# A trunk layer's first microseconds: raw x turned ahead of its norm, and the last x tile moved behind the first modulation

## The chip, the cores and the metric

One core of a Trainium2 chip runs the whole program. The time is the device time of that core in microseconds (us). The kernel before was timed in three runs. The engines are called TensorE (PE), VectorE (DVE), ScalarE (ACT), GpSimd (POOL) and SyncE (SP); SP issues nearly all transfers.

## What is computed

One layer of a hybrid backbone for 640 tokens of width 1024: 128 context tokens and 512 latent ones. Cut to what the change touches:

```python
def rms_norm(x, g):
    xf = x.astype(jnp.float32)
    y = xf * lax.rsqrt(jnp.mean(xf * xf, axis=-1, keepdims=True) + EPS)
    return (y * g.astype(jnp.float32)).astype(x.dtype)

def trunk_layer(h, ada, p, rope_tabs, ctx_k, ctx_v):
    sh1, sc1, g1, sh2, sc2, g2 = jnp.split(ada, N_ADA, axis=-1)
    u = rms_norm(h, p["g_pre1"]) * (1 + sc1) + sh1
    mo, k, v = mixer(u, p, rope_tabs, ctx_k, ctx_v)
    h = h + g1 * rms_norm(mo, p["g_post1"])
    u = rms_norm(h, p["g_pre2"]) * (1 + sc2) + sh2
    h = h + g2 * rms_norm(conv_ffn(u, p), p["g_post2"])
    return h, k, v
```

Here `ada` is silu(c) @ w_ada + b_ada, and the mixer begins with z = u @ w_in. All numbers are 32-bit floats. Products that must be exact to that are made of three products of parts: a weight or an activation is split into a high part (rounded to a narrower format, names in `whi`, `UH`) and the low rest (`wlo`, `UL`), and high x high, high x low and low x high are added up.

## The kernel before

TensorE contracts over the 128 partitions, so the modulated u is needed with features on the partitions and tokens along the row: `UH` and `UL`, eight feature blocks f of 128 features by 640 tokens. x comes from memory the other way round, in five tiles t of 128 tokens by 1024 features (`XT`; tile 0 is the context, 1 to 4 are latent).

What happens to x, ahead of the first matmul with real weights (called the prologue here):

- `square(t)`: ScalarE squares the tile and sums each row; GpSimd makes the factor 1/sqrt(mean + EPS) of it in two small steps (`rstd_of`, lines 224 and 225), one number for each token, that is for each partition.
- `normal(t)`: VectorE multiplies the tile by that factor (line 358).
- `x_turn(t)`: TensorE turns the product in eight transposes of 128x128 into PSUM (line 365).
- `x_copy(t, half)`: VectorE or ScalarE copies each half to `xT` (lines 371 and 373).

Beside this stands the modulation. Scale and shift of a feature block are sums over w_ada. Its columns are loaded in groups g (`GROUPS`: the feature blocks 0; 1; 2 and 3; 4 and 5; 6; 7), `ada1_mm(g, i)` multiplies them (i = 0 is the scale, i = 1 the shift; line 383), `ada1_copy` takes the result from PSUM on ScalarE (line 390, tile `e`), and `ada1_fold` adds up its four partial rows on TensorE (line 397) and makes `scsh` on VectorE (lines 400 and 402). `modulate(f, a, b)` then makes `UH` on ScalarE (line 417), the same in full precision on VectorE (`u`, line 418) and `UL` (line 421) for the tokens a to b. `features` and `feature_columns` turn the small vectors (c, biases, gains) into columns; the first needs four small loads that ScalarE issues.

With a modulated block f and a weight block f of w_in (K and V columns, "unit" f, split by `split`, lines 148 and 149, which `cut_upto` calls), `kv_mm(f, ts)` adds block f to the K/V result of the token tiles ts: three matmuls of 128x512 each (lines 183 to 185). `kv_first` does the same for block 0 and three tiles, ordered so that the low parts are needed last (line 428).

The order on TensorE, ScalarE, VectorE and SP is the order of the calls in the text: the engines' programs are written out by hand, and each is worked through in that order, so an instruction that waits holds up all that stands behind it on its engine. SP issues the loads in their order in the text, and at most eight are under way; the places freed by x tiles 0 to 4 take later w_ada groups (`ada_loads(2, ...)`, `ada_loads(3, ...)`). PSUM tiles come from two rings: three of two banks (`ps2`: the turned tiles, then the K/V results) and two of one bank (`ps1`: `wps` for the first transposes, `features`, then each `ada1_mm` group).

At the very start 28 transposes of the identity run on TensorE (`WARM`, line 298).

After the last `kv_mm` come attention, the convolution, the merge and the feed-forward part, in which nothing is edited.

Of the kernel before, what the change touches and what calls it, by code (L numbers as in the profile page):

```python
# [11 lines left out]
F32 = mybir.dt.float32  # L12
F32R = mybir.dt.float32r
AF = mybir.ActivationFunctionType
ALU = mybir.AluOpType
# [22 lines left out]
OFF = 192  # L38
BLKS = ((0, 320), (320, 640))
ZB = 4  # L40
XB = 4
WARM = 28
SEGS = ((0, NCTX), (NCTX, NTOK))


# [18 lines left out]
def trunk_layer(ctx, tc, x_prompt, x_sample, cache_k, cache_v, c, c_ctx, w_ada, b_ada, g_pre1, g_post1, g_pre2,  # L64
# [29 lines left out]
    def nm(s):  # L94
        cnt[0] += 1
        return f"{s}_{cnt[0]}"
# [19 lines left out]
    def ps2():  # L116
        return ps.tile([128, 1024], F32, tag="s2", name=nm("s2"), bufs=3)
# [36 lines left out]
    def fetch(i):  # L154
        while len(state["raw"]) < min(i, len(units), state["limit"]):
            w, k0, nk, c0, n = units[len(state["raw"])]
            if nk * n > 512:
                raw = raw_tile()
            else:

                if not halves:
                    raw = raw_tile()
                    halves.extend([raw[:, 512:1024], raw[:, 0:512]])
                raw = halves.pop()
            nc.sync.dma_start(raw[:, :nk * n].rearrange("p (k c) -> p k c", c=n),
                              w[k0 * 128:(k0 + nk) * 128, c0:c0 + n].rearrange("(k p) c -> p k c", p=128))
            state["raw"].append(raw)
# [125 lines left out]
    with tc.tile_pool(name="pro", bufs=2) as pro, tc.manual_schedule(engines={mybir.EngineType.SP}):  # L293
        warm = pro.tile([128, 1], F32, name="warm", bufs=1)
        S.activation(warm, mhalf[:, 0:1], AF.Silu)
        wps = ps1()
        for _ in range(WARM):
            PE.transpose(wps[:, 0:128], ident, ident)

        def load_rows(srcs, eng):  # L300
            rows = pro.tile([72, 128], F32, tag="rows", name=nm("rows"), bufs=2)
# [13 lines left out]
        def araw_tile():  # L315
            return pro.tile([128, 1024], F32, tag="araw", name=nm("araw"), bufs=4)

        def ada_loads(g, rooms):
            n, c = len(GROUPS[g]), GROUPS[g][0] * 128
            araws[g] = rooms  # L320
            for i, raw in enumerate(rooms):
                o, k = (D, 0)[i // n], i % n * (KT // n)
                nc.sync.dma_start(raw.rearrange("p (k c) -> p k c", c=128 * n),
                                  w_ada[k * 128:(k + KT // n) * 128, o + c:o + c + 128 * n].rearrange("(k p) c -> p k c", p=128))

        XT = region(ra, "r3", [NT, D], F32, "XT")
        for t in range(NT):
            nc.sync.dma_start(XT[:, t, :], xrows(t))
        ada_loads(0, [araw_tile() for _ in range(2)])
        fetch(1)  # L330
        ada_loads(1, [araw_tile() for _ in range(2)])
        fetch(2)

        def features():
            ptr = ps1()
            PE.transpose(ptr[:, 0:72], rows1, ident[0:72, 0:72])
            S.activation(svec[:, :, 30], ptr[:, 0:8], AF.Silu)
            S.activation(svec[:, :, 31], ptr[:, 8:16], AF.Silu)
            return ptr

        def feature_columns():
            V.tensor_copy(feat[:, 0:72], ptr1[:, 0:72])
            for o in (8, 32):
                V.tensor_scalar(out=feat[:, F_B + o:F_B + o + 8], in0=feat[:, F_B + o:F_B + o + 8], scalar1=1.0, scalar2=None,
                                op0=ALU.add)

        xT = Halves(NTOK, F32, "xT")
        xns, rs, xps, pas, es = {}, {}, {}, {}, {}

        def square(t):  # L350
            junk = pro.tile([128, D], F32, tag="junk", name=nm("junk"), bufs=1)
            ssq = pro.tile([128, 1], F32, tag="ssq", name=nm("ssq"), bufs=NT)
            S.activation(junk, XT[:, t, :], AF.Square, accum_out=ssq)
            rs[t] = rstd_of(ssq, 1, 1.0 / D, pro)

        def normal(t):
            xns[t] = pro.tile([128, D], F32, tag="xn", name=nm("xn"), bufs=XB)
            V.tensor_scalar(out=xns[t], in0=XT[:, t, :], scalar1=rs[t], scalar2=None, op0=ALU.mult)

        def x_turn(t, ks=range(KT)):  # L360
            if ks[0] == 0:
                xps[t] = ps2()
            p = xps[t]
            for k in ks:
                PE.transpose(p[:, k * 128:(k + 1) * 128], xns[t][:, k * 128:(k + 1) * 128], ident)

        def x_copy(t, hf):
            src = xps[t].rearrange("p (k c) -> p k c", c=128)[:, 4 * hf:4 * hf + 4]
            dst = xT.half(hf)[:, :, t * 128:(t + 1) * 128]
            if t > 0 and hf == 0:  # L370
                S.activation(dst, src, AF.Copy)
            else:
                V.tensor_copy(dst, src)

        def ada1_mm(g, i):

# [43 lines left out]
                x()  # L420
            V.tensor_tensor(out=UL[:, f, a:b], in0=u[:, a:b], in1=UH[:, f, a:b].bitcast(F32), op=ALU.subtract)

        def kv_first(ts):

            wh, wl = state["cut"][0].at(0)
            for x, w in ((UH, wh), (UH, wl), (UL, wh)):
                for t in ts:
                    PE.matmul(kvp[t], x[:, 0, t * 128:(t + 1) * 128], w, start=x is UH and w is wh, stop=False)

        def kv_mm(f, ts):  # L430
            for t in ts:
# [19 lines left out]
            V.tensor_tensor(out=kl, in0=p, in1=kh.bitcast(F32), op=ALU.subtract)  # L451


        for t in range(2):
            square(t)
        normal(0)
        square(2)
        x_turn(0)
        normal(1)
        square(3)  # L460
        ptr1 = features()
        x_turn(1)
        x_copy(0, 0)
        normal(2)
        square(4)
        x_copy(0, 1)
        x_copy(1, 0)
        x_turn(2)
        normal(3)
        ada_loads(2, [XT[:, t, :] for t in range(4)])  # L470
        fetch(3)
        x_turn(3)
        x_copy(2, 0)
        feature_columns()
        x_copy(1, 1)
        ada1_mm(0, 0)
        ada1_mm(0, 1)
        normal(4)
        x_copy(2, 1)
        x_copy(3, 0)  # L480
        ada1_copy(0)
        x_copy(3, 1)
        x_turn(4, range(4))
        ada1_fold(0)
        x_turn(4, range(4, KT))

        whi, wlo = (wp.tile([128, 1024], F32R, tag=x, name=nm(x), bufs=3)[:, 0:512] for x in ("whi", "wlo"))
        raw = state["raw"][0][:, 0:512]
        S.activation(whi, raw, AF.Copy)
        state["cut"].append(Unit((whi, wlo), 512))  # L490
        modulate(0, 0, 512, [lambda: V.tensor_tensor(out=wlo, in0=raw, in1=whi.bitcast(F32), op=ALU.subtract)])
        x_copy(4, 0)
        x_copy(4, 1)
        kv01, kv23, kv4a = ps2(), ps2(), ps2()
        kvp = [kv01[:, 0:512], kv01[:, 512:1024], kv23[:, 0:512], kv23[:, 512:1024], kv4a[:, 0:512]]

        def ada1(g):
            for i in range(2):
# [1 line left out]
            ada1_copy(g)  # L500


        ada1_mm(1, 0)
        kv_first((0, 1, 2))
        modulate(0, 512, NTOK)
        cut_upto(2)
        ada1_mm(1, 1)
        ada1_copy(1)
        ckrt = araw_tile()
        fetch(5)  # L510
        ada_loads(3, [XT[:, 4, :]] + [araw_tile() for _ in range(3)])
        kv_mm(0, (3,))
        ada1_fold(1)
        kv_mm(0, (4,))
        modulate(1, 0, 384)
        modulate(1, 384, NTOK)
        ada1_mm(2, 0)
        ada1_copy(2, 0, 1)
        kv_mm(1, (0, 1))
        ada1_mm(2, 1)  # L520
        cut_upto(3)
        ada1_copy(2, 1, 2)
        fetch(6)
        kv_mm(1, (2,))
        ada1_fold(2, (0,))
        kv_mm(1, (3, 4))
        modulate(2, 0, 384)
        modulate(2, 384, NTOK)
        ada1_fold(2, (1,))
# [1570 lines left out]
```

## Time and profile before

| | us |
|---|---|
| median of three runs | 1118.98 |
| lowest and highest run | 1118.9, 1119.33 |
| the profiled execution | 1120.78 |
| its span, first to last instruction | 1118.7 |

In that span TensorE is busy for 1105.9 us, VectorE for 795.6, ScalarE for 575.2 and GpSimd for 147.4. The page cuts the span into 40 slices of 28 us; the change lies in the first of them and a little of the second.

How to read the rows below. A timeline row has start, duration, engine, line, operation, tile written <- tiles read, shape, and in brackets how long the engine sat idle before and what ended that. PEld is TensorE's weight load, which overlaps its matmuls; a transposition counts as a matmul. A matmul's duration includes its way through the array, so matmuls that overlap start closer than their durations. A row of a chain has start, duration and what. A row of busy time by stretch has the stretch, its length, then for each engine the busy us and the count of instructions, then the granted TensorE clock, the mean busy share of the DMA engines, and GB/s. A row of a group has line, engine, operation, tiles, shapes and count, then busy us in all and mean ns of one.

### The profile page before, as it was taken

The page shows a single profiled execution, that of the slowest core. Times are in us where ns is not written, and L with a number is a line of the kernel's source. Part 1 is how long each engine was busy: PE and PEld are TensorE (multiplying, and loading weights), DVE is VectorE, ACT ScalarE, POOL GpSimd, SP SyncE. Part 2 cuts the span into 40 slices and gives each one's busy share as a digit, 9 for nine tenths or more (in the row PEclk, how much of TensorE's full clock was granted, in tenths as well). Part 3 has the DMA queues.
Part 4 walks back from the last instruction along what each step waited for, and adds up shares of the span by engine and source line. Part 5 has one row for each costly group of instructions (what it writes and reads, how often), then busy time and mean ns, then how long its engine had stood idle before and what let it go on. Part 6 is the DMA issues. An engine that isn't in the chain of part 4 may idle for free.

```text
span 1118.7 us, 19626 instructions
## 1 busy us (share of the span) xinstructions
PE 1105.9 (99%) x7893; PEld 1016.6 (91%) x7893; DVE 795.6 (71%) x1303; ACT 575.2 (51%) x1015; POOL 147.4 (13%) x191
## 2 busy tenths in 40 slices
PE   8999999999999999999999999999999999999997
PEld 5798888888999999999999889999999999998786
DVE  5687667664646798889645457888888888889544
ACT  5476766655235444545522257554655455556431
POOL 1056566652000000000000012000000000000001
PEclk9999999999999999999999999999999999999999
DMA  9844323323222223223332644232333233315722
GB/s 317 237 124 133 95 76 96 108 82 114 77 76 76 76 83 105 78 76 95 95 105 73 221 145 156 71 113 92 118 106 99 91 108 107 118 62 180 263 90 94
DMA packets 177448, 129.58 MB, mean 116 GB/s; under 512 B 6290, under 2 KB 159822, under 8 KB 177358
## 3 DMA queue, kind: packets, MB, share of 16 engines
q1 hardware_dynamic: 177246, 128.30, 37.4%
q8 instruction: 62, 1.02, 0.4%
q14 instruction: 28, 0.23, 0.1%
q10 hardware_dynamic: 112, 0.04, 0.0%
HBM read 116.87 MB, written 11.45 MB: 115 GB/s over the span
## 4 chain that ended last, share of the span: by engine, by line
PE 95%; DMA 2%; ACT 1%; DVE 1%; issue 0%; POOL 0%; POOLq 0%; DVEq 0%; SPq 0%; ACTq 0%
PE b L1143 45%; PE b L185 9%; PE b L183 9%; PE b L184 9%; PE s L862 3%; PE s L672 3%; PE s L886 3%; PE s L183 3%; PE s L185 3%; PE s L184 3%; DMA raw<-in_w_in_dram 1%; PE s L235 1%; DMA araw<-in_w_ada_dram 1%; PE b L1680 1%; DMA XT<-in_x_sample_dram 0%; PE s L643 0%
## 5 line engine op out<-in xcount | busy, mean ns | idle before, releaser
L1143 PE MATMUL b<-ZB,whi 128*128 128x320 f32 x1024 | 226.0, 309 | 0.0
L1143 PEld LDWEIGHTS b<-ZB,whi 128*128 128x128 f32 x1024 | 171.9, 188 | 1.8
L1143 PE MATMUL b<-ZB,wlo 128*128 128x320 f32 x512 | 158.0, 309 | 0.0
L1143 PE MATMUL b<-MT,whi 128*128 128x320 f32 x608 | 134.2, 309 | 0.0
L1143 PEld LDWEIGHTS b<-MT,whi 128*128 128x128 f32 x608 | 101.6, 188 | 0.0
L1143 PEld LDWEIGHTS b<-ZB,wlo 128*128 128x128 f32 x512 | 96.2, 188 | 0.0
L1143 PE MATMUL b<-MT,wlo 128*128 128x320 f32 x304 | 93.9, 309 | 0.0
L849 POOL TENSOR_TENSOR pr<-pr,sm 128x640 f32<-128x640 f32 x64 | 80.0, 1260 | 58.8 <-DVE sm L848 56.5
L1130 ACT ACTIVATE whi<-SUM 128x1024 fp32r<-128x1024 f32 x40 | 42.2, 1055 | 77.4 <-DVE SUM L1595 74.8
L1625 DVE SCALAR_TENSOR_TENSOR Y<-C,cffn,Y 128x642 f32<-128x642 f32 x88 | 77.7, 883 | 0.9
L839 ACT ACTIVATE pr<-s,mx,rq 128x640 f32<-128x640 f32 x64 | 56.6, 884 | 33.0 <-DVE mx L826 30.9
L149 DVE TENSOR_TENSOR wlo<-raw,whi 128x1024 fp32r<-128x1024 f32 (+1 forms) x32 | 35.4, 1106 | 53.0 <-ACT whi L148 49.4
L1143 PE MATMUL b<-UL,whi 128*128 128x320 f32 x228 | 70.9, 311 | 0.0
L1143 PE MATMUL b<-UH,wlo 128*128 128x320 f32 x228 | 70.0, 307 | 0.0
L1143 PE MATMUL b<-UH,whi 128*128 128x320 f32 x228 | 69.4, 304 | 0.0
L1130 ACT ACTIVATE whi<-WB 128x1024 fp32r<-128x1024 f32 x38 | 40.1, 1055 | 55.7 <-DVE WB L1238 55.7
L1134 DVE TENSOR_TENSOR wlo<-raw,whi 128x1024 fp32r<-128x1024 f32 (+1 forms) x51 | 50.5, 1020 | 25.2 <-ACT whi L1130 24.3
L183 PE MATMUL s<-whi,UH 128*128 128x256 f32 (+1 forms) x197 | 63.9, 324 | 0.0
L821 DVE TENSOR_REDUCE mx<-s 128x1 f32<-128x640 f32 x64 | 52.5, 820 | 15.6 <-PE s L672 15.0
L1151 ACT ACTIVATE p<-b 128x320 f32<-128x320 f32 x78 | 34.2, 438 | 53.9 <-PE b L1143 52.0
L185 PE MATMUL s<-whi,UL 128*128 128x256 f32 (+1 forms) x197 | 59.9, 304 | 0.0
L184 PE MATMUL s<-wlo,UH 128*128 128x256 f32 (+1 forms) x197 | 59.6, 303 | 0.0
(346 smaller groups left out, 2916.3 us busy)
## 6 DMA issues: line engine op xcount, KB each, us to landing
raw<-in_w_in_dram SPq DMA_DIRECT2D x48, 512.0 KB, 3.6
RAW<-in_w_up_dram SPq DMA_DIRECT2D x40, 512.0 KB, 4.0
raw<-in_w_ada_dram SPq DMA_DIRECT2D x30, 512.0 KB, 4.3
raw<-in_w_down_dram SPq DMA_DIRECT2D x22, 512.0 KB, 5.1
actd<-Y SPq DMA_DIRECT2D x18, 321.0 KB, 2.7
XT<-in_w_ada_dram SPq DMA_DIRECT2D x9, 512.0 KB, 6.8
raw<-in_w_conv_out_dram SPq DMA_DIRECT2D x9, 512.0 KB, 4.6
raw<-in_w_att_out_dram SPq DMA_DIRECT2D x8, 512.0 KB, 4.1
```

The source lines that it names most:

```text
L149: V.tensor_tensor(out=lo[:, :n], in0=raw, in1=hi[:, :n].bitcast(F32), op=ALU.subtract)
L183: PE.matmul(out, ah, bh, start=start, stop=False)
L184: PE.matmul(out, ah, bl, start=False, stop=False)
L185: PE.matmul(out, al, bh, start=False, stop=stop)
L821: V.tensor_reduce(out=mx, in_=self.sc[h], axis=AX.X, op=ALU.max, negate=True)
L839: S.activation(pr, self.sc[h], AF.Exp, bias=mx, scale=rs, accum_out=sm)
L849: G.tensor_tensor(out=pr, in0=pr, in1=sm.broadcast_to((128, NTOK)), op=ALU.mult)
L1130: S.activation(to[0], raw, AF.Copy)
L1134: V.tensor_tensor(out=lo, in0=raw, in1=hi.bitcast(F32), op=ALU.subtract)
L1143: PE.matmul(out, p[:, ws], q[:, k, :], start=start and k == 0 and n == 0, stop=stop and k == 3 and n == 2, skip_group_check=True)
L1151: S.activation(t, pair[j][b], AF.Copy)
L1625: V.scalar_tensor_tensor(out=y, in0=crows(j)[i][:, d:d + NACT], scalar=cffn[:, 44 * d + o:44 * d + o + 1], in1=y, op0=ALU.mult, op1=ALU.add)
```

## The change

The tile that is turned is x as it lands: `x_turn` reads `XT`, and `normal` is gone. The factors, one for each partition, are spread over 128 columns and turned as well (`r_turn`), so that they stand as a row, the same in all partitions. `x_copy` copies that row from PSUM and VectorE multiplies both halves of the turned tile by it on the way to `xT`; ScalarE copies none. The factor turns use the PSUM tile `wps` of the first transposes. The 28 transposes of the identity become six, and two lots of four come later (`idle`). The last x tile is loaded behind group 0 of w_ada and the first weight unit, turned behind the fold of group 0, squared behind the first modulation, and multiplied behind the first nine K/V matmuls. The nine matmuls' order of `kv_first` is used for feature block 1, too, ahead of group 2's `ada1_mm`. Some calls around them change places: `ada1_mm(1, 0)` goes behind `kv_first`, `modulate(0, 512, NTOK)` and `cut_upto(2)` behind group 1's copy, and `cut_upto(3)` behind group 2's.

```diff
@@ -38,8 +38,7 @@
 OFF = 192
 BLKS = ((0, 320), (320, 640))
 ZB = 4
-XB = 4
-WARM = 28
+WARM = 6
 SEGS = ((0, NCTX), (NCTX, NTOK))
 
 
@@ -294,8 +293,12 @@
         warm = pro.tile([128, 1], F32, name="warm", bufs=1)
         S.activation(warm, mhalf[:, 0:1], AF.Silu)
         wps = ps1()
-        for _ in range(WARM):
-            PE.transpose(wps[:, 0:128], ident, ident)
+
+        def idle(n):
+            for _ in range(n):
+                PE.transpose(wps[:, 384:512], ident, ident)
+
+        idle(WARM)
 
         def load_rows(srcs, eng):
             rows = pro.tile([72, 128], F32, tag="rows", name=nm("rows"), bufs=2)
@@ -324,10 +327,11 @@
                                   w_ada[k * 128:(k + KT // n) * 128, o + c:o + c + 128 * n].rearrange("(k p) c -> p k c", p=128))
 
         XT = region(ra, "r3", [NT, D], F32, "XT")
-        for t in range(NT):
+        for t in range(NT - 1):
             nc.sync.dma_start(XT[:, t, :], xrows(t))
         ada_loads(0, [araw_tile() for _ in range(2)])
         fetch(1)
+        nc.sync.dma_start(XT[:, NT - 1, :], xrows(NT - 1))
         ada_loads(1, [araw_tile() for _ in range(2)])
         fetch(2)
 
@@ -345,7 +349,7 @@
                                 op0=ALU.add)
 
         xT = Halves(NTOK, F32, "xT")
-        xns, rs, xps, pas, es = {}, {}, {}, {}, {}
+        rs, xps, pas, es = {}, {}, {}, {}
 
         def square(t):
             junk = pro.tile([128, D], F32, tag="junk", name=nm("junk"), bufs=1)
@@ -353,24 +357,23 @@
             S.activation(junk, XT[:, t, :], AF.Square, accum_out=ssq)
             rs[t] = rstd_of(ssq, 1, 1.0 / D, pro)
 
-        def normal(t):
-            xns[t] = pro.tile([128, D], F32, tag="xn", name=nm("xn"), bufs=XB)
-            V.tensor_scalar(out=xns[t], in0=XT[:, t, :], scalar1=rs[t], scalar2=None, op0=ALU.mult)
-
-        def x_turn(t, ks=range(KT)):
-            if ks[0] == 0:
-                xps[t] = ps2()
-            p = xps[t]
-            for k in ks:
-                PE.transpose(p[:, k * 128:(k + 1) * 128], xns[t][:, k * 128:(k + 1) * 128], ident)
-
-        def x_copy(t, hf):
-            src = xps[t].rearrange("p (k c) -> p k c", c=128)[:, 4 * hf:4 * hf + 4]
-            dst = xT.half(hf)[:, :, t * 128:(t + 1) * 128]
-            if t > 0 and hf == 0:
-                S.activation(dst, src, AF.Copy)
-            else:
-                V.tensor_copy(dst, src)
+        def x_turn(t):
+            p = xps[t] = ps2()
+            for k in range(KT):
+                PE.transpose(p[:, k * 128:(k + 1) * 128], XT[:, t, k * 128:(k + 1) * 128], ident)
+
+        def r_turn(t):
+
+            PE.transpose(wps[:, t % 3 * 128:t % 3 * 128 + 128], rs[t].broadcast_to((128, 128)), ident)
+
+        def x_copy(t):
+
+            row = pro.tile([128, 128], F32, tag="row", name=nm("row"))
+            V.tensor_copy(row, wps[:, t % 3 * 128:t % 3 * 128 + 128])
+            for hf in range(2):
+                V.tensor_tensor(out=xT.half(hf)[:, :, t * 128:(t + 1) * 128],
+                                in0=xps[t].rearrange("p (k c) -> p k c", c=128)[:, 4 * hf:4 * hf + 4],
+                                in1=row.unsqueeze(1).broadcast_to((128, 4, 128)), op=ALU.mult)
 
         def ada1_mm(g, i):
 
@@ -420,12 +423,12 @@
                 x()
             V.tensor_tensor(out=UL[:, f, a:b], in0=u[:, a:b], in1=UH[:, f, a:b].bitcast(F32), op=ALU.subtract)
 
-        def kv_first(ts):
-
-            wh, wl = state["cut"][0].at(0)
+        def kv_first(f, ts):
+
+            wh, wl = state["cut"][f].at(0)
             for x, w in ((UH, wh), (UH, wl), (UL, wh)):
                 for t in ts:
-                    PE.matmul(kvp[t], x[:, 0, t * 128:(t + 1) * 128], w, start=x is UH and w is wh, stop=False)
+                    PE.matmul(kvp[t], x[:, f, t * 128:(t + 1) * 128], w, start=f == 0 and x is UH and w is wh, stop=False)
 
         def kv_mm(f, ts):
             for t in ts:
@@ -451,48 +454,42 @@
             V.tensor_tensor(out=kl, in0=p, in1=kh.bitcast(F32), op=ALU.subtract)
 
 
-        for t in range(2):
-            square(t)
-        normal(0)
+        square(0)
+        square(1)
+        x_turn(0)
+        x_turn(1)
+        ptr1 = features()
+        r_turn(0)
+        x_copy(0)
         square(2)
-        x_turn(0)
-        normal(1)
+        x_turn(2)
         square(3)
-        ptr1 = features()
-        x_turn(1)
-        x_copy(0, 0)
-        normal(2)
-        square(4)
-        x_copy(0, 1)
-        x_copy(1, 0)
-        x_turn(2)
-        normal(3)
+        r_turn(1)
+        feature_columns()
+        x_copy(1)
+        x_turn(3)
         ada_loads(2, [XT[:, t, :] for t in range(4)])
         fetch(3)
-        x_turn(3)
-        x_copy(2, 0)
-        feature_columns()
-        x_copy(1, 1)
+        r_turn(2)
+        x_copy(2)
         ada1_mm(0, 0)
+        r_turn(3)
+        x_copy(3)
+        idle(4)
         ada1_mm(0, 1)
-        normal(4)
-        x_copy(2, 1)
-        x_copy(3, 0)
         ada1_copy(0)
-        x_copy(3, 1)
-        x_turn(4, range(4))
-        ada1_fold(0)
-        x_turn(4, range(4, KT))
 
         whi, wlo = (wp.tile([128, 1024], F32R, tag=x, name=nm(x), bufs=3)[:, 0:512] for x in ("whi", "wlo"))
         raw = state["raw"][0][:, 0:512]
         S.activation(whi, raw, AF.Copy)
         state["cut"].append(Unit((whi, wlo), 512))
+        idle(4)
+        ada1_fold(0)
+        x_turn(4)
         modulate(0, 0, 512, [lambda: V.tensor_tensor(out=wlo, in0=raw, in1=whi.bitcast(F32), op=ALU.subtract)])
-        x_copy(4, 0)
-        x_copy(4, 1)
-        kv01, kv23, kv4a = ps2(), ps2(), ps2()
-        kvp = [kv01[:, 0:512], kv01[:, 512:1024], kv23[:, 0:512], kv23[:, 512:1024], kv4a[:, 0:512]]
+        square(4)
+        kv01, kv23 = ps2(), ps2()
+        kvp = [kv01[:, 0:512], kv01[:, 512:1024], kv23[:, 0:512], kv23[:, 512:1024]]
 
         def ada1(g):
             for i in range(2):
@@ -500,30 +497,33 @@
             ada1_copy(g)
 
 
+        kv_first(0, (0, 1, 2))
+        r_turn(4)
+        x_copy(4)
+        kvp.append(ps2()[:, 0:512])
         ada1_mm(1, 0)
-        kv_first((0, 1, 2))
-        modulate(0, 512, NTOK)
-        cut_upto(2)
         ada1_mm(1, 1)
         ada1_copy(1)
         ckrt = araw_tile()
         fetch(5)
         ada_loads(3, [XT[:, 4, :]] + [araw_tile() for _ in range(3)])
+        modulate(0, 512, NTOK)
         kv_mm(0, (3,))
         ada1_fold(1)
+        cut_upto(2)
         kv_mm(0, (4,))
         modulate(1, 0, 384)
         modulate(1, 384, NTOK)
+        kv_first(1, (0, 1, 2))
         ada1_mm(2, 0)
         ada1_copy(2, 0, 1)
-        kv_mm(1, (0, 1))
         ada1_mm(2, 1)
+        ada1_copy(2, 1, 2)
         cut_upto(3)
-        ada1_copy(2, 1, 2)
         fetch(6)
-        kv_mm(1, (2,))
+        kv_mm(1, (3,))
         ada1_fold(2, (0,))
-        kv_mm(1, (3, 4))
+        kv_mm(1, (4,))
         modulate(2, 0, 384)
         modulate(2, 384, NTOK)
         ada1_fold(2, (1,))
```

## The prediction

> **What bounds the kernel now.** I read the page first: busy shares, and the slices of 28 us.
>
> ```profile
> PE 1105.9 (99%) x7893; PEld 1016.6 (91%) x7893; DVE 795.6 (71%) x1303; ACT 575.2 (51%) x1015; POOL 147.4 (13%) x191
> DMA  9844323323222223223332644232333233315722
> GB/s 317 237 124 133 95 76 96 108 82 114 77 76 76 76 83 105 78 76 95 95 105 73 221 145 156 71 113 92 118 106 99 91 108 107 118 62 180 263 90 94
> ```
>
> TensorE is busy 99% of the span, and only in the first slice are the DMA engines full (317 GB/s). The edit lies in that slice, so I then took busy time by stretch, the chain of waits of the first 32 us, and the timeline.
>
> ```profile
> 20.00:32.00 12.00, 11.57 (x88) 6.86 (x87) 6.23 (x17) 5.67 (x12) 0.00 (x0) 1.00 1.09 362
> 32.00:59.00 27.00, 27.00 (x204) 20.61 (x203) 18.55 (x51) 13.33 (x22) 0.00 (x0) 1.00 0.78 223
> ...
> 1.19 5.28 DMA XT<-in_x_sample_dram
> 6.49 8.19 DMA araw<-in_w_ada_dram
> 17.01 1.10 ACT UH L417 x2
> 18.23 9.32 DMA raw<-in_w_in_dram
> 27.58 0.63 ACT whi L148
> 28.21 0.28 ACT e L390
> 28.54 0.61 PE s L397 x4
> ```
>
> First number of the upper rows after the length: TensorE. It has no gap from 32 to 59 us, and the DMA share falls there from 1.09 to 0.78. So up to about 32 us the loads lead, after that TensorE does. The chain says the same: x until 6.47, the first w_ada block until 14.68, then the third K/V weight block (unit 2 of w_in), which lands at 27.55. The timeline shows where the lead passes over.
>
> ```profile
> 26.93 0.16 PEld L383 LDWEIGHTS s<-XT,s 128*32 128x32 f32 x8 [0.48 <-DMA XT<-in_w_ada_dram]
> 28.24 0.69 DVE L149 TENSOR_TENSOR wlo<-raw,whi 128x512 fp32r<-128x512 f32 x1 [2.60 <-ACT whi L148]
> 29.25 0.28 DVE L400 TENSOR_SCALAR scsh<-s,feat 128x2 f32<-128x2 f32 x1 [0.32 <-PE s L397]
> 29.70 1.48 ACT L417 ACTIVATE UH<-xTa,scsh 128x128 fp32r<-128x128 f32 x3 [1.21 <-DVE scsh L402]
> 30.71 0.56 DVE L421 TENSOR_TENSOR UL<-u,UH 128x384 fp32r<-128x384 f32 x1 [0.35 <-ACT UH L417]
> 31.33 0.19 PEld L185 LDWEIGHTS s<-whi,UL 128*128 128x128 f32 x1 [0.21 <-DVE UL L421]
> ```
>
> The 31.33 row is TensorE's last wait before the dense stretch; call that instant M. Behind M both kernels hold the same instructions in the same order on every engine, so what the edit is worth is the shift of M. The times above M are one series: the last quarter of the third w_ada group lands at 26.93, unit 2 at 27.55, scale and shift of feature block 2 at 29.25, its low half at 30.71.
>
> **Loads.** The last x tile moves behind the first w_ada block and unit 0. At 317 GB/s its 0.52 MB are 1.65 us: the first block lands near 13.0 instead of 14.68, unit 0 as much earlier. From the second w_ada block on, the same bytes lie ahead of each load, so 26.93 and 27.55 stay. The later loads into the x region now wait for transposes instead of VectorE.
>
> ```profile
> 15.43 2.75 SPq L323 DMA_DIRECT2D XT<-in_w_ada_dram  x4
> 22.36 0.38 SPq L323 DMA_DIRECT2D XT<-in_w_ada_dram  x1
> 17.21 0.38 PEld L383 LDWEIGHTS s<-araw,s 128*32 128x32 f32 x16 [0.48 <-DMA araw<-in_w_ada_dram]
> ```
>
> Tiles 0 to 3 are turned by about 12.5 and tile 4 by 17.6 (below), ahead of 15.43 and 22.36: no cost on SP. If tile 3's turn came after 17.4, SP would hold back unit 2 behind it.
>
> **Turning and scaling.** Rows for the prices:
>
> ```profile
> 5.10 1.06 ACT L353 ACTIVATE junk<-XT 128x1024 f32<-128x1024 f32 x1 [2.87 <-DMA XT<-in_x_prompt_dram]
> 6.61 0.55 POOL L225 TENSOR_TENSOR rstd<-var,mhalf 128x1 f32<-128x1 f32 x1
> 7.19 0.75 DVE L358 TENSOR_SCALAR xn<-XT,rstd 128x1024 f32<-128x1024 f32 x1 [5.21 <-POOL rstd L225]
> 8.00 1.09 PE L365 MATMUL s<-ident,xn 128*128 128x128 f32 x8 [1.30 <-DVE xn L358]
> 8.93 0.23 PE L336 MATMUL s<-ident,rows 72*128 72x72 f32 x1
> 12.27 0.23 DVE L342 COPY feat<-s 128x72 f32<-128x72 f32 x1
> 14.17 1.28 DVE L373 COPY xTb<-s 128x512 f32<-128x512 f32 x2
> L371 ACT ACTIVATE xTa<-s 128x512 f32<-128x512 f32 x4 | 2.2, 584 | 0.2 <-PE s L365 0.2
> L451 DVE TENSOR_TENSOR KL<-s,KH 128x512 fp32r<-128x512 f32 x1 | 0.7, 684 | 0.0
> L256 DVE COPY tabk<-s x2: 279/285/291, 66.1 to 168.6; 128x128 f32<-128x128 f32 x2
> ```
>
> Removed: five multiplications of 0.75 us on VectorE, four copies of 0.58 on ScalarE, six of 0.68 on VectorE. Added per tile: one transpose for the factor, a 128x128 copy out of PSUM (0.29), and two products of 512 with PSUM as input, for which I take the 0.684 of KL. Two copies of that length start 0.60 apart (1.28 less 0.68), so a tile holds VectorE 0.3 + 0.6 + 0.6 = 1.5 us, all of it after its factor. The four tiles ahead of the first modulation make 6.0 us, and feature_columns some 0.5 between them (its copy 0.23, two small steps as much again).
>
> New waits: each factor turn writes one PSUM bank and must wait for the row copy before it; the four idle transposes in front of the second half of the first w_ada block wait for tile 3's row copy. So that half, landed at 13.0, queues on TensorE behind VectorE. Likewise the turn of factor 4 stands ahead of both halves of the second w_ada block, the third K/V tile and the fold behind them.
>
> **The clock at the start.** 22 of 28 warm-up transposes go.
>
> ```profile
> L298 PE MATMUL s<-ident 128*128 128x128 f32 x11 | 2.6, 423 | 1.6 <-POOL ident masks.py:199 1.6
> ```
>
> This is the window from 1 to 4 us: eleven from 1.63 on, so 0.22 us apart; the eight of the 8.00 row stand 0.11 apart. Some time between, TensorE doubled its rate. With six transposes and then 2 us of nothing, the x tiles meet either rate: 1.1 us for eight, or 1.8 at the early one. Where the early one holds, tiles 0 to 2 keep TensorE dense from 5.1. The old dense run began at 1.63 and had doubled by 8.0, between 2.4 and 6.4 us after its start; so the early rate would end between 7.5 and 11.5, and I take 10.
> The Trainium skill, TensorE: Matmul & The Clock Gate, Part 1, has the clock double after some 3.4 us of sustained work; by that the dense run from 5.1 ends the slow rate between 8.5 and 12. Its Part 4 says that transposes don't count as work for this; here the rate rose with nothing but transposes on TensorE, so they do.
>
> **The schedule, fast (slow).** The second x tile, landed at 6.47, is turned by 7.6 (8.7). The feature rows follow; their small loads are in by 8.93, where the old row names no wait for them, and I let this turn end at 8.2 (8.75). Factor 0, ready since 7.2, comes next, its row copy at 8.4 (9.1). VectorE is then in one piece: 1.5 for tile 0, 0.5, 3.0 for tiles 1 and 2, some 0.2 of gaps, and row copy 3 starts at 13.6 (14.3). Behind it the idle transposes end at 14.35, the half block (0.64) at 15.0, the copy e (0.36) at 15.4, the fold (0.61) at 16.0: scale and shift 16.1 (16.8), and 0.45 later the first UH, 16.6 (17.3) against 17.01 in the old chain. So the 1.65 us of the load are spent on VectorE's row of products.
> The nine first K/V matmuls need the low halves, too; the last three started 2.44 after UH (19.45 below) and hold TensorE for 0.71, so they end at 19.75 (20.45). ScalarE's square of tile 4 comes behind the first UH, so factor 4 is ready at 19.5 (20.2). Behind its turn the two half blocks (the first landed by 17.21, the other one transfer, 1.65, later) run until 21.15 (21.9); in the old order the second of them ran at the same time:
>
> ```profile
> 20.24 0.64 PE L383 MATMUL s<-araw,s 128*32 128x128 f32 x16
> 23.22 1.48 ACT L417 ACTIVATE UH<-xTa,scsh 128x128 fp32r<-128x128 f32 x3 [1.21 <-DVE scsh L402]
> 26.29 1.28 PE L383 MATMUL s<-XT,s 128*32 128x256 f32 x16
> 28.12 0.36 ACT L390 ACTIVATE e<-s 128x256 f32<-128x256 f32 x1
> 18.74 0.87 PE L428 MATMUL s<-wlo,UH 128*128 128x512 f32 x3
> 19.45 0.86 PE L428 MATMUL s<-whi,UL 128*128 128x512 f32 x3
> ```
>
> Products of tile 4, its modulation, the fold: UH of block 1 at 22.95 (23.65) against 23.22. Now nine matmuls come ahead of the third w_ada group instead of six, 0.71 more; they end at 25.55 (26.3). The group's 2.6 us end at 28.2 (28.95); the old ones ended at 27.57 with the landing. Its copy e no longer stands behind whi of unit 2 on ScalarE, but whi now stands behind it: whi 28.55 (29.3), wlo 29.2 (29.95), scale and shift 29.8 (30.55) against 29.25, and 2.1 later, as before, the low half's matmul: 31.9 (32.65) against 31.33. TensorE has less left to do meanwhile (tile 2 is done), so it waits about 1 us there: the tile put ahead gives nothing back.
>
> **Sum.** M moves by +0.6 with the fast start and by +1.3 with the slow one; I take the middle, +0.95, since nothing tells which rate six transposes leave. Behind M nothing absorbs it: 27 us of dense TensorE. The profiled execution took 1120.78 for its span of 1118.7; the median of the runs is 1118.98, so I put the shift on that: 1119.9, with 1119.3 to 1120.5 for this case.
>
> **Rivals.**
> No change: VectorE's chain is shorter than I make it (the products start closer, the bank waits cost nothing), and the loads at 26.93 and 27.55 lead again. Then e at 27.6, whi 27.9, scale and shift 29.2, M at 31.25: 1118.9, between 1118.7 and 1119.1. For it speaks that 0.6 us less in the whole chain is enough; against it the row copies in front of TensorE.
> Faster: the loads themselves arrive earlier because the start no longer waits on tile 4. If all of the 1.65 reached M, and e escaping whi's 0.54 too (28.12 against 27.58), it is 1118.98 - 2.2 = 1116.8. Against it: DMA share of 1.09 to 32 us, which no order of the same bytes makes shorter.
> Slower: the low rate stays through the first dense K/V work, as the gaps from 12 to 17 us are too many.
>
> Then on the path: four idle transposes +0.4, a half block +0.4, the fold +0.2, tile 4's turn +0.5, nine matmuls of 0.24 each doubled +2.1, two half blocks +0.7: up to 4.3 on top of 1.3. Some 1 us of it is hidden, where tile 4's turn and the fold run while VectorE or ScalarE is awaited, so 1123.6; if the rate rises in the midst of the nine matmuls, half, 1121.6. It decides if the rate hasn't risen when the half block starts near 14 us.
>
> **How the numbers follow.** My forecast 0.56, no change 0.20, faster 0.06, slower by the rate 0.18. The time is the forecast's, 1119.9. The range takes in the no-change case whole with half a us to spare, 1118.2, and the slow case to the middle of the nine matmuls and a little beyond, 1121.9; outside it lie the faster case and the worst of the slow one, some 0.16. A measurement of this kernel tells about 0.2%, 2.2 us, from no change: forecast and no-change case lie within, with a little of both others. Faster by more 0.05, within 0.78, slower by more 0.17.
>
> **What would show it.** Right: VectorE in one piece from about 8.5 to 16, the half of the first w_ada block starting 1 us or more after its landing, the third group's matmuls ending after 27.6, a wait of about 1 us ahead of the third K/V block's matmuls, M at 31.9 to 32.65. No change: M within 0.1 of 31.33 with the group's landing as the last wait. Slow rate: matmuls of 512 columns that start over 0.4 apart near 18 us. Wrong altogether: unit 2 landing at another time than 27.55, or TensorE no longer dense behind M.

## The result and the profile after

| | us |
|---|---|
| changed kernel, median of ten runs (lowest, highest) | 1121.74 (1121.22, 1123.16) |
| kernel before, ten runs beside them | 1119.10 (1118.90, 1119.85) |
| ratio and its 95% interval | 1.0024 (1.0015 to 1.0032) |
| profiled execution of the changed kernel, its span | 1121.34, 1119.2 |

The change costs 2.64 us, a little over the 0.2% that a measurement tells from no change. The time was forecast at 1119.9; 1121.74 lies near the upper end of the range, and above the 1119.3 to 1120.5 that the forecast gave for its own case.

Busy time by stretch in the changed kernel (stretch, length, then busy time of TensorE, weight loads, VectorE, ScalarE, GpSimd, the granted clock, DMA share, GB/s):

```profile
20.00:32.00 12.00, 11.19 (x101) 7.07 (x99) 6.94 (x19) 5.33 (x12) 0.00 (x0) 1.00 1.09 360
32.00:59.00 27.00, 26.64 (x202) 20.34 (x202) 18.46 (x51) 13.67 (x23) 0.00 (x0) 1.00 0.72 205
```

TensorE still has only small gaps, and the second stretch loses 0.36 us, because its first wait now lies behind 32 us. The loads are as dense as before (1.09). What changed is who leads. Here is the chain of waits of the changed kernel's first 33 us (start, length, what):

```profile
0.73 3.70 DMA XT<-in_x_prompt_dram
...
4.47 3.67 PE s L363 x16
...
23.43 2.61 PE s L431 x9
26.04 1.04 PE s L386 x16
27.12 0.04 issue
27.17 0.39 ACT e L393
27.61 1.11 PE s L386 x16
28.74 0.38 ACT e L393
29.13 0.53 ACT whi L147
29.68 0.69 DVE wlo L148
30.37 0.19 DVE scsh L403
```

Before, three loads were in this chain: x, the first w_ada block and the third K/V weight block (unit 2). Now only the first x tile is. From 4.47 on the chain is work: transposes, VectorE's products, the nine first K/V matmuls of each block, then the two halves of the third w_ada group with their copies `e`, and unit 2's split behind them. Unit 2 has been in SBUF for 2.6 us when `whi` reaches it at 29.02 (the last of its landing events in the trace is at 26.45). The same in the timeline (start, length, engine, line, operation; in brackets the idle time before it and what ended that):

```profile
8.52 0.29 DVE L372 COPY row<-s 128x128 f32<-128x128 f32 x1 [6.53 <-PE s L367]
13.50 0.28 DVE L372 COPY row<-s 128x128 f32<-128x128 f32 x1
13.84 0.66 PE L299 MATMUL s<-ident 128*128 128x128 f32 x4 [1.14 <-DVE row L372]
16.74 1.09 ACT L420 ACTIVATE UH<-xTa,scsh 128x128 fp32r<-128x128 f32 x2 [0.70 <-DVE scsh L405]
27.61 1.07 PE L386 MATMUL s<-XT,s 128*32 128x256 f32 x16 [0.56 <-ACT e L393]
29.02 0.62 ACT L147 ACTIVATE whi<-raw 128x512 fp32r<-128x512 f32 x1
30.29 0.28 DVE L403 TENSOR_SCALAR scsh<-s,feat 128x2 f32<-128x2 f32 x1
32.35 0.19 PEld L184 LDWEIGHTS s<-whi,UL 128*128 128x128 f32 x1 [0.79 <-DVE UL L424]
```

The last row is M, TensorE's last wait before the dense stretch: 32.35, against 31.33 in the profiled execution of before. That is only 1.02 later, although the medians lie 2.64 apart. The first experiment asks what 31.33 was worth.

### The profile page after: what moved, and what is told of

Its sections match the earlier page's. It is cut to its first block, busy times and chain, and to the rows that moved or that the text cites. A ratio compares the mean times of both kernels' runs of the same rounds, so it can differ in the third digit from the quotient of the medians.

```text
span 1119.2 us, 19605 instructions
## 1 busy us (share of the span) xinstructions
PE 1105.7 (99%) x7884; PEld 1016.8 (91%) x7884; DVE 795.4 (71%) x1307; ACT 573.5 (51%) x1011; POOL 146.9 (13%) x191
## 3 DMA queue, kind: packets, MB, share of 16 engines
q8 instruction: 62, 1.02, 0.4%
## 4 chain that ended last, share of the span: by engine, by line
PE 97%; DVE 2%; ACT 1%; DMA 0%; issue 0%; POOL 0%; POOLq 0%; DVEq 0%; ACTq 0%
PE b L1143 45%; PE b L184 9%; PE b L182 9%; PE b L183 9%; PE s L672 3%; PE s L886 3%; PE s L862 3%; PE s L182 3%; PE s L184 3%; PE s L183 3%; PE s L234 1%; PE b L1680 1%; PE s L386 1%; PE s L643 0%; PE s L431 0%; PE b L1531 0%
```

## Experiments

Each time stands against the kernel before, timed beside it on the same chip; "over before" is the difference of these two medians. Each interval is about 1 us wide to either side, so differences of a few tenths between runs are readings of medians that the intervals alone don't show.

| run | median (lowest, highest) | over before | ratio, 95% interval |
|---|---|---|---|
| the change | 1121.74 (1121.22, 1123.16) | +2.64 | 1.0024 (1.0015 to 1.0032) |
| e0, before again | 1119.08 (1118.64, 1119.62) | +0.01 | 0.9998 (0.999 to 1.0007) |
| e1, change with 28 warm-ups | 1121.86 (1121.45, 1123.68) | +2.79 | 1.0027 (1.0016 to 1.0038) |
| e2, change with the old order | 1119.96 (1119.04, 1121.37) | +0.89 | 1.0009 (0.9999 to 1.0018) |
| e3, change, copies last | 1121.30 (1120.93, 1122.99) | +2.23 | 1.0021 (1.0011 to 1.0031) |
| e4, before with the new order | 1119.92 (1119.34, 1121.21) | +0.99 | 1.0009 (1.0 to 1.0017) |
| e5, e2 with idle transposes | 1119.20 (1118.59, 1119.86) | +0.27 | 1.0002 (0.9993 to 1.0011) |
| e6, before, copies first | 1118.27 (1118.10, 1119.13) | -0.66 | 0.9993 (0.9984 to 1.0001) |
| e7, change with idle transposes | 1121.42 (1120.86, 1121.97) | +2.49 | 1.0019 (1.001 to 1.0028) |
| e9, e5, copies first | 1119.67 (1119.22, 1119.86) | +0.59 | 1.0005 (0.9996 to 1.0014) |
| e10, e7, first half back | 1120.31 (1119.99, 1120.82) | +1.23 | 1.001 (1.0002 to 1.0019) |

### e0: where M of a typical execution of before lies

The kernel before, unchanged, for another profile.

> The kernel before, unchanged, for a second profile of it. Its profiled execution took 1120.78 us, 1.7 above the median of its runs, and the changed kernel's profiled execution (1121.34) was near its own median (1121.74). Theory A (the loss lies ahead of the dense stretch, and the first profile of before was held up by late loads): this profile, if its time is near 1119, shows the third K/V block's weights landing 1 to 2 us earlier than 27.55 and the last wait ahead of the dense stretch near 29.6 in place of 31.33. Theory B (the loss lies behind that wait, as the two profiles differ by only 1.0 there): the wait stays at 31.3 within 0.4. Time: 1.000 of before.

Its profiled execution took 1119.15 us, close to the median. Its timeline:

```profile
15.57 1.09 ACT L417 ACTIVATE UH<-xTa,scsh 128x128 fp32r<-128x128 f32 x2 [0.68 <-DVE scsh L402]
26.27 0.63 ACT L148 ACTIVATE whi<-raw 128x512 fp32r<-128x512 f32 x1 [2.41 <-DMA raw<-in_w_in_dram]
26.81 0.36 ACT L390 ACTIVATE e<-s 128x256 f32<-128x256 f32 x1
27.94 0.28 DVE L400 TENSOR_SCALAR scsh<-s,feat 128x2 f32<-128x2 f32 x1 [0.32 <-PE s L397]
30.02 0.19 PEld L185 LDWEIGHTS s<-whi,UL 128*128 128x128 f32 x1 [0.22 <-DVE UL L421]
```

Unit 2 is there 1.3 us earlier than in the profile that the prediction used, and M is at 30.02 instead of 31.33. So the change moves M by 2.33 in a typical execution, and the two spans (1117.1 and 1119.2) differ by 2.1. (M gives the time to some tenths only: from M to the end of the span the twelve traces take 1086.5 to 1087.3 us.) The first `UH` starts at 15.57, so against this execution the changed prologue is 1.17 later (16.74), where it is 0.27 earlier than the 17.01 in the prediction's trace. The 31.33 belonged to an execution of 1120.78 whose loads came late. The chain of the changed kernel doesn't contain these loads.

### e1: the warm-up

```diff
-WARM = 6
+WARM = 28
```

> The changed kernel with 28 transposes at the start in place of 6. Theory A1 (VectorE's chain of products and the order of blocks 1 and 2 cost the time; the slow rate of TensorE at the start only moves the feature rows and the first factor): 0.2 to 0.7 us off 1121.74, so 1121.0 to 1121.5. Theory A2 (the rate at the start is what costs): back to 1119.1 to 1119.6.

Nothing is gained: +2.79 against +2.64, where 0.2 to 0.7 was expected. With 28 warm-ups the clock is at 1.0 from 5.24 us, and the time stays. The profile fell on the slowest execution (1123.68), which shows something else; its stretches:

```profile
12.00:15.00 3.00, 1.43 (x25) 0.93 (x21) 2.93 (x7) 0.00 (x0) 0.00 (x0) 1.00 1.11 352
15.00:22.00 7.00, 7.00 (x33) 5.96 (x26) 2.54 (x7) 3.03 (x6) 0.74 (x2) 0.53 1.12 339
```

From 12 to 15 us TensorE works for 1.43 of 3 us, and then the granted clock falls: 0.5 from 15.48 to 22.31 us in the trace's clock records, a mean of 0.53 in this stretch. The three matmuls of the first K/V tiles with `wlo`, in this trace and then in that of the changed kernel:

```profile
19.56 1.48 PE L431 MATMUL s<-wlo,UH 128*128 128x512 f32 x3
```

```profile
18.45 0.86 PE L431 MATMUL s<-wlo,UH 128*128 128x512 f32 x3
```

The clock was up, and it fell again.

### e2: the old order of the second and third feature block

```diff
-        kv_first(1, (0, 1, 2))
         ada1_mm(2, 0)
         ada1_copy(2, 0, 1)
+        kv_mm(1, (0, 1))
         ada1_mm(2, 1)
-        ada1_copy(2, 1, 2)
         cut_upto(3)
+        ada1_copy(2, 1, 2)
         fetch(6)
-        kv_mm(1, (3,))
+        kv_mm(1, (2,))
         ada1_fold(2, (0,))
-        kv_mm(1, (4,))
+        kv_mm(1, (3, 4))
```

> The changed kernel with the old order from group 2 of w_ada on: two K/V tiles of block 1 between the two halves of the group, three behind it, and unit 2's split ahead of the second copy. Theory A1: the new order costs about half of the loss (nine matmuls in place of six ahead of the group, and the group's second half waiting for the copy of the first): 1.0 to 1.4 us off 1121.74, 1120.3 to 1120.7. Theory A2 or a loss made wholly ahead of block 1: within 0.3 of 1121.74.

Of the 2.64, 1.75 go, more than the 1.0 to 1.4 expected, and 0.89 is left. The profiled execution (1119.04) has M back at 30.36. `whi` waits for its load again, but the chain of waits holds no load behind the first x tile: from 17.9 us on it runs through TensorE.

```profile
26.20 0.63 ACT L147 ACTIVATE whi<-raw 128x512 fp32r<-128x512 f32 x1 [1.49 <-DMA raw<-in_w_in_dram]
30.36 0.19 PEld L184 LDWEIGHTS s<-whi,UL 128*128 128x128 f32 x1 [0.22 <-DVE UL L424]
```

But the runs spread from 1119.04 to 1121.37. The seven with a mean granted clock of 0.996 or 0.997 took 1119.58 to 1121.37, the four at 0.998 or 0.999 took 1119.04 to 1119.51.

### e3: the copies of the third group behind both halves

```diff
         ada1_mm(2, 0)
-        ada1_copy(2, 0, 1)
         ada1_mm(2, 1)
+        ada1_copy(2, 0, 1)
         ada1_copy(2, 1, 2)
```

> The changed kernel with both copies of group 2 behind both of its halves, so that the second half doesn't wait for the first copy (0.56 us of idle TensorE in the profile of the changed kernel). Theory A1: that wait is on the path, 0.4 to 0.6 us off 1121.74, 1121.1 to 1121.35. If the wait only takes the place of another: within 0.15 of 1121.74.

It gains 0.41 to 0.44, as expected; between the executions with a granted clock of 0.998 or more alone, seven of each, it is 0.53 (1121.66 to 1121.13). That is less than an interval can show, but it fits: the wait of 0.56 in the 27.61 row is on the path. The second half writes other columns than the copy reads, but of the same PSUM tile, one bank.

### e4: the new order alone

The kernel before with the order of the change from block 1 on; the prologue stays as it was. (`kv_first` takes the block as an argument, as in the change; that part of the edit is left out here.)

```diff
+        kv_first(1, (0, 1, 2))
         ada1_mm(2, 0)
         ada1_copy(2, 0, 1)
-        kv_mm(1, (0, 1))
         ada1_mm(2, 1)
-        cut_upto(3)
         ada1_copy(2, 1, 2)
+        cut_upto(3)
         fetch(6)
-        kv_mm(1, (2,))
+        kv_mm(1, (3,))
         ada1_fold(2, (0,))
-        kv_mm(1, (3, 4))
+        kv_mm(1, (4,))
```

> The kernel before with one part of the change only: the order of the second and third feature block's work (nine K/V matmuls of block 1 ahead of the third w_ada group, the copies e of the group ahead of whi of unit 2). Theory A (the new order by itself holds the third block's scale and shift back: the group's two halves lie behind nine matmuls instead of six, the second half waits for ScalarE's copy of the first, whi waits for e): in an execution whose unit 2 lands near 26.2 us, e of the second half ends about 28.1 to 28.5, scale and shift of block 2 start near 29.5 to 29.9 against 27.94, the last wait of TensorE comes near 31.5 to 32, the time is 1120.5 to 1121.0 (+1.4 to +1.9). Rival B (the order costs only behind the changed prologue, whose chain is later from the start): the last wait stays within 0.4 of 30.02, the time is 1119.0 to 1119.5.

+0.99 lies between the two expectations. The mechanism is there, but smaller:

```profile
22.29 1.22 PE L428 MATMUL s<-whi,UH 128*128 128x512 f32 x3 [0.30 <-ACT UH L417]
26.42 1.07 PE L383 MATMUL s<-XT,s 128*32 128x256 f32 x16 [0.50 <-ACT e L390]
31.17 0.19 PEld L185 LDWEIGHTS s<-whi,UL 128*128 128x128 f32 x1 [0.79 <-DVE UL L421]
```

The same wait for the copy, and M at 31.17, 1.15 behind e0. The nine matmuls start at 22.29 here and at 23.50 in e7, behind the changed prologue: 1.21 apart.

### e5 and e7: idle transposes where TensorE stood idle

Twelve more transposes, written into columns of the first group's PSUM tile that nothing reads; the waits for the row copies stay. e5 adds them to e2, e7 to the change itself.

```diff
+        def fill(n):
+            for _ in range(n):
+                PE.transpose(pas[0][:, 256:384], ident, ident)
...
         ada1_mm(0, 0)
+        fill(4)
         r_turn(3)
         x_copy(3)
+        fill(8)
         idle(4)
```

> The changed kernel with the old order from the third w_ada group on, and with 12 more idle transposes between 12 and 14 us, written into a part of PSUM that no row copy reads, so that TensorE doesn't stand idle there; the waits for the row copies stay. Theory C (the 0.9 us that the old order alone left comes from executions in which TensorE's clock falls to half near 15 us, because TensorE has stood idle too much before): no execution shows a mean granted clock under 0.998, and the median is 1119.0 to 1119.4. Rival D (it is a delay in every execution, of the chain or the loads): the median stays at 1119.8 to 1120.2, with clocks as they come.

> The changed kernel with the same 12 idle transposes between 12 and 14 us and its new order kept. Theory C: what is left is the delay of the new order, in every execution: clocks at 0.998 or more, median 1121.0 to 1121.4 with a narrower spread than 1121.22 to 1123.16. Rival D: as the changed kernel, 1121.6 to 1121.9.

The medians came out as the clock theory has them, e7 0.02 above its upper edge. The 12 to 15 us stretch of the changed kernel, then of e7:

```profile
12.00:15.00 3.00, 1.46 (x22) 0.93 (x22) 2.93 (x7) 0.00 (x0) 0.00 (x0) 1.00 1.11 352
```

```profile
12.00:15.00 3.00, 2.74 (x37) 2.15 (x33) 2.93 (x7) 0.00 (x0) 0.00 (x0) 1.00 1.11 351
```

With TensorE busy for 2.74 of the 3 us, none of the 22 executions of e5 and e7 shows a mean clock under 0.998; of the 21 of the change and e2, ten did. In time this is worth 0.62 with the old order (+0.89 to +0.27) and 0.15 with the new one (+2.64 to +2.49); the second is too small to be shown by medians alone.

The pair also gives the price of the order behind the changed prologue: +2.49 less 0.27 is 2.22. What it consists of stands in e5's timeline:

```profile
23.03 1.07 PE L390 MATMUL s<-XT,s 128*32 128x256 f32 x16
24.64 0.19 PEld L184 LDWEIGHTS s<-whi,UL 128*128 128x128 f32 x1 [0.31 <-DVE UL L428]
25.77 1.07 PE L390 MATMUL s<-XT,s 128*32 128x256 f32 x16
26.91 0.39 ACT L397 ACTIVATE e<-s 128x256 f32<-128x256 f32 x1 [0.25 <-PE s L390]
```

In the old order the group's first half runs at 23.03, while `UH` and `UL` of block 1 are being made; its second half starts at 25.77. In e7 the nine matmuls start at 23.50, the first half comes behind them at 26.04, and the second at 27.67:

```profile
23.50 1.22 PE L435 MATMUL s<-whi,UH 128*128 128x512 f32 x3 [0.23 <-ACT UH L424]
26.04 1.07 PE L390 MATMUL s<-XT,s 128*32 128x256 f32 x16
27.67 1.07 PE L390 MATMUL s<-XT,s 128*32 128x256 f32 x16 [0.56 <-ACT e L397]
32.42 0.19 PEld L184 LDWEIGHTS s<-whi,UL 128*128 128x128 f32 x1 [0.79 <-DVE UL L428]
```

### e6: the copies ahead of unit 2's split, in the kernel before

```diff
         ada1_mm(2, 1)
-        cut_upto(3)
         ada1_copy(2, 1, 2)
+        cut_upto(3)
```

> The kernel before with the copy e of the third w_ada group's second half ahead of whi of unit 2 on ScalarE, nothing else. In the kernel before, whi (26.27 to 26.9) stands ahead of e (26.81), while the group's matmuls end near 26.3. Theory: scale and shift of block 2 start 0.2 to 0.5 earlier, at 27.45 to 27.75 (wlo, 0.69 on VectorE, then comes ahead of them and limits the gain), and the time is 1118.6 to 1119.0. Rival: wlo, later by whi's delay, holds scale and shift back by as much, and the time is 1119.1 to 1119.4.

The median lies 0.66 below before, more than expected; the interval (0.9984 to 1.0001) just holds 1, though nine of the eleven executions are faster than the fastest (1118.52) of the 33 of before. If the gain is real, this is the part of the change's order that helps, and the fastest kernel here. Its profiled execution (1119.13) is its slowest, with late loads again (unit 2 at 26.75), so its instants can't be set against e0's.

### e9 and e10: the terms taken one by one

e10 is e7 with the first half, and its copy, back ahead of the nine matmuls:

```diff
-        kv_first(1, (0, 1, 2))
         ada1_mm(2, 0)
         ada1_copy(2, 0, 1)
+        kv_first(1, (0, 1, 2))
```

> The kernel e7 (the change with 12 idle transposes more) with the first half of the third w_ada group and its copy e back ahead of the nine K/V matmuls of block 1; the nine stay in one piece, and whi of unit 2 stays behind both copies. Theory A, by terms: the first half (1.07) fills TensorE's wait for UH and UL of block 1 instead of standing behind the nine, and its copy e is long done when the second half comes, so the wait of 0.56 goes too; the second half starts near 26.5 instead of 27.67, e near 27.6 instead of 28.81, the last wait comes near 31.2 to 31.4 instead of 32.42, the time is 1120.2 to 1120.6. Rival E (what holds is whi and wlo of unit 2 behind the copies, not the matmuls): under 0.4 gained, 1121.0 to 1121.5.

+1.23 against +2.49: the gain is 1.26, as expected, and so are the instants:

```profile
26.54 1.07 PE L390 MATMUL s<-XT,s 128*32 128x256 f32 x16
27.68 0.38 ACT L397 ACTIVATE e<-s 128x256 f32<-128x256 f32 x1 [2.84 <-PE s L390]
31.29 0.19 PEld L184 LDWEIGHTS s<-whi,UL 128*128 128x128 f32 x1 [0.79 <-DVE UL L428]
```

The second half starts at 26.54 instead of 27.67 and M comes at 31.29 instead of 32.42. e9 is e5 with the swap of e6, same diff:

> The kernel e5 (old order, changed prologue, 12 idle transposes more) with both copies e of the third w_ada group ahead of whi of unit 2, as in e6. Theory F (behind the changed prologue TensorE's chain leads even in the old order: in e5's trace whi, 26.03 to 26.66, is done before e can start at 26.91): the swap gains nothing, and wlo, now later, holds scale and shift back to about 28.6 against 28.19: 1119.2 to 1119.7. Rival G (the loads lead, and the prologue has slack as in the kernel before): as in e6, 0.5 to 0.7 less than e5: 1118.4 to 1118.8.

The swap that gained 0.66 in the kernel before costs 0.32 here:

```profile
27.29 0.39 ACT L397 ACTIVATE e<-s 128x256 f32<-128x256 f32 x1 [2.29 <-PE s L390]
27.57 0.62 ACT L147 ACTIVATE whi<-raw 128x512 fp32r<-128x512 f32 x1
28.22 0.69 DVE L148 TENSOR_TENSOR wlo<-raw,whi 128x512 fp32r<-128x512 f32 x1 [2.40 <-ACT whi L147]
28.83 0.27 DVE L407 TENSOR_SCALAR scsh<-s,feat 128x2 f32<-128x2 f32 x1
```

In e5 `e` waited for TensorE, not for `whi` (which ran from 26.03 to 26.66), so there is nothing to gain, and `wlo`, now later, stands in front of scale and shift. In the kernel before `e` stood behind `whi`. Behind the changed prologue TensorE is thus as late as the loads, even in the old order, and e5's chain of waits, like e2's, holds no load behind the first x tile: no slack is left.

## Why the prediction was right or wrong

**The schedule was right.** VectorE in one piece from 8.5 (8.52), row copy 3 at 13.6 (13.50), the first `UH` at 16.6 (16.74), the group's end at 28.2 to 28.95 (28.68), scale and shift of block 2 at 29.8 to 30.55 (30.29), M at 31.9 to 32.65 (32.35). The early rate of TensorE, said to end between 7.5 and 11.5, ended at 8.02 to 10.84 in the seven traces with six transposes. The second half of the first w_ada block queued behind row copy 3 and the idle transposes (13.84 row), and what was won on the loads was spent on VectorE, as forecast.

**The step that failed is the baseline under the sum.** "M moves by +0.6 with the fast start and by +1.3 with the slow one" subtracts 31.33, and "I put the shift on that" adds the difference to a median which isn't this execution's. In e0, an execution of the median, M is at 30.02: with it the same schedule gives +1.9 to +2.6, thus 1120.9 to 1121.6. The text saw that the profiled execution was 1.8 us above the median, but not what that meant: its loads were late, before was led by these loads, and the changed kernel is not. A lateness of the loads cancels in the difference only if both kernels wait for them. That 1121.74 still lies in the range is luck: the range reached up to 1121.9 for the low rate of TensorE, and filling the gaps that let the rate fall gave back only 0.15 of the 2.64.

**Nine matmuls ahead of the group.** Priced at "0.71 more", the three matmuls that stand ahead of the second half in addition. The order behind this prologue costs 2.22 (e7 less e5). Half of it, 1.26, is the first half that left TensorE's wait for block 1 (e10), with the wait for its copy that came with it; e3 puts 0.41 on that wait, which the prediction didn't have. The remaining 0.96 (e10 less e5: 1.23 less 0.27) fits the three matmuls (0.71) and `whi` and `wlo` behind the copies, but wasn't taken apart further. "The tile put ahead gives nothing back" held: TensorE waits 0.79 at M.

**Two parts that don't add up.** The new order alone costs 0.99 (e4), the prologue with the old order 0.27 (e5), both 2.49 (e7): 1.23 more than the sum. The changed prologue brings the nine matmuls 1.21 later (22.29 to 23.50). In the old order the delay is nearly all taken up by the time that TensorE's chain had in hand ahead of the loads (M at 30.27 in e5, 30.02 in e0); with the new order nothing is in hand, and all of it counts. The sizes fit, but the runs don't take this apart further.

**The rivals.** The "no change" rival has its time in e5 (1119.20), the change without its new order, but not its cause: there TensorE leads, not the loads. "Slower by the rate" was half right: the low rate does strike the first K/V matmuls in part of the executions, and "the gaps from 12 to 17 us" are the place, since filling them ends it. Its condition was wrong: the rate had risen long before 14 us and fell again. Its price was too high for the median, 0.15 to 0.62 instead of 1.7 to 3.7 over the forecast, as most executions escape; the slowest, 1123.16 at a clock of 0.995, lies near the 1123.6 given, but by another sum: the fall costs it about 1.5 us over the 1121.66 of the undisturbed executions, not 3.3 over 1120.3. (On that base half the price would have been 1121.9, not the 1121.6 given.) The start itself (six transposes or 28) costs nothing that e1 shows.

**Loads.** The sign "unit 2 landing at another time than 27.55", one of those of being wrong altogether, came: it landed at 26.45 in the changed kernel. Against e0's 26.25 the load hardly moved, so what was wrong was the instant taken from one late execution. In the changed kernel it no longer matters: in e7 it lands at 25.99, and M comes at 32.42.

## What to carry to other kernels

Before a shift read from one trace is put on a median, ask whether the execution's lateness lies on the changed kernel's path, too; a second trace of the kernel before would have moved this forecast by 1.3 us. Work that fills an engine's wait isn't free to move: put behind that wait it costs its whole length, and two edits that are each hidden by the same slack can cost when they come together. Where one PSUM tile takes two results in turn, copy it out after both, or early enough that the second doesn't wait for the copy of the first.

## What the runs showed of the hardware

**The clock falls though every gap is short.** In e1 and e3 the granted clock was 1.0 from 5.24 and 8.02 us on and went to 0.5 at 15.48 and 14.84, for 6.83 us each time (the trace's clock records). The longest idle time of TensorE named in any of these traces between 9 and 15 us is 1.14 us (the 13.84 row). But it was busy for only about half of 12 to 15 us. The profiled execution of the change had 1.46 busy of the same 3 us and kept its clock, so a stretch like this goes either way from one execution to the next; with 2.74 of 3 in the traces of e5 and e7, none of their 22 executions shows a mean clock that such a fall would leave.

The Trainium skill, TensorE: Matmul & The Clock Gate, Part 1, lets the clock drop after an idle window of about 3.4 us (3413 ns), and has that window run freely: it doesn't reset when a kernel starts. Two such windows would be 6.83 us (an estimate from that figure), as measured, and every stretch between two changes of the clock in the twelve traces is a whole number of 3.413 us: two and three at 1.0 ahead of the falls, two at 0.5, and 321 to 325 in the long ones. So which execution is struck can depend on where the windows' borders fall; this is argued, as the unprofiled executions show no borders. What makes a window count as idle stays open. Here is the one that ended in e3's fall, one that the changed kernel passed at 1.0, and e3's last one with matmuls, at whose end the clock stayed at 1.0:

```profile
11.43:14.84 3.41, 1.85 (x37) 1.06 (x28) 3.34 (x7) 0.00 (x0) 0.26 (x1) 1.00 1.09 355
12.19:15.61 3.42, 2.07 (x26) 1.39 (x26) 2.85 (x6) 0.47 (x2) 0.00 (x0) 1.00 1.12 333
1113.94:1117.35 3.41, 0.56 (x3) 0.12 (x1) 1.82 (x4) 0.69 (x2) 0.75 (x2) 1.00 0.33 121
```

A window need not be idle throughout for a fall, and TensorE's busy time alone doesn't decide either. The Trainium skill, TensorE: Matmul & The Clock Gate, Part 4, by which transposes don't count as work for the clock in the same way, doesn't hold here: e5 and e7 differ from e2 and the change in twelve transposes alone, and these kept the clock up.

**In these programs matmuls wait for a copy out of other columns of their PSUM bank**: 0.50 to 0.56 us in three kernels (the rows at 26.42, 27.61 and 27.67). The Trainium skill, PSUM — Partial Sum Buffer, PSUM bank collisions raise a hardware error, says that two engines must not touch one bank and partition quadrant at once, even in different columns, so that the program has to order them. The rows agree with such an order; what would happen without it wasn't tried.
